# The first head group's inverse roots: eight rows through device memory in place of spreading transposes

## The chip, the cores and the metric

The kernel runs on one core of a Trainium2 chip. A core has a matrix engine (PE in the profile, with PEld for its weight loads), three engines for elementwise work (DVE, ACT and POOL), and an engine that mostly issues transfers (SP). Each engine takes its instructions in order and waits on semaphores for the others. The metric is the device time of one execution in microseconds. Three executions of the kernel before took 1020.29, 1020.35 and 1021.29 us; the median is 1020.35 us.

## The reference

One encoder layer on 1024 tokens of width 1024, all in float32. Two attention groups of eight heads each work on one projection; each group's output is normalised by the root mean square over its 512 columns before the shared output projection. A gated MLP follows. Only the first group's normalisation is touched by the change.

```
hn   = rmsnorm(h, norm_mix)
proj = einsum('bsd,de->bse', hn, w_in)
qa, ka, va, qb, kb, vb = split(proj)
o_a  = window_gqa_sink(rope(qa), rope(ka), va, sink)     # 8 heads of 64, window 128
o_b  = neighbourhood_attention(qb, kb, vb, rpb)          # 8 heads of 64, 16 x 64 grid
mix  = concatenate([rmsnorm(o_a, norm_a), rmsnorm(o_b, norm_b)])
h    = h + einsum('bse,ed->bsd', mix, w_out)
h    = h + conv_gated_mlp(rmsnorm(h, norm_ffn), ...)
out  = rmsnorm(h, norm_final)
```

with `rmsnorm(x, g) = x * rsqrt(mean(x * x) + 1e-6) * g`. For the first group that is, for each token, 1 / sqrt(sum of 512 squares / 512 + 1e-6): 1024 numbers, one for each token.

## The kernel before

Activations are kept transposed: 128 features on the partitions, 1024 tokens along the free axis. `mix[0:4]` are the four tiles of the first group's output, `mix[4:8]` those of the second. Scaling the tiles by a number per token therefore needs that number in all 128 partitions: a tile of 128 x 1024 in which every row is the same. This tile is `norm["a"]` (`rstda` in the profile).

Every float32 product is made of three matmuls with rounded high parts and remainders (`block`, L178 to L180), so PE has much to do. The order of PE's instructions is the order of the program text (`manual_schedule`). On the other engines a planner orders the work: it places each instruction when its inputs are ready by the planner's own reckoning of durations, and among ready ones takes the earlier in the program, with `tc.high_priority(offset=500)` pulling one ahead.

PE's text is an interleaving of two streams. The attention units make scores, transposes and value products. The generator `rest()` yields projection blocks, one k tile for one half of the tokens at a time, and `fill(n)` puts n of these blocks between attention steps. `jobs[i]` are 15 projections (column tiles 3 to 17) followed by eight output projections; a job has 16 blocks, 8 for each half. Small pieces of other work hang on places in this stream: `aux[i, n]` is called after block n of job i, just ahead of the next block. "(12, 5)" below is such a place.

For the first group, these pieces are, in the kernel before:

- (11, 8) `square_a`: `squares` (L193, L195) squares the four `mix` tiles on ACT and adds them on DVE, in halves, into a tile of the pool `t` that has three buffers.
- (12, 2) and (12, 5) `narrow_a`: `add_up` transposes 4 blocks of 128 x 128 of the sum on PE (L204) into a PSUM bank and reduces them on DVE (L205), so that the sums of 512 tokens stand in 4 columns of `norm["v"]`, a tile of 128 x 8. After the second half `inverse_root` (L208) takes the square root on ACT and the reciprocal on DVE.
- (12, 11) and (12, 13) `wide_a`: `widen` makes 4 transposes on PE of a column that is repeated 128 times (L235), which leaves the 512 numbers in every partition of a PSUM bank; ACT copies it to `norm["a"]` (L828).
- (13, 1) to (13, 12) `normed_a`: eight multiplications on DVE, each a half of a `mix` tile (L832).

The PSUM banks of `narrow_a` and `wide_a` carry the tag `pj`, of which there are two. The projection uses the same two: the first half of a job accumulates in one during blocks 0 to 7, the second in the other during blocks 8 to 15, and `evacuate` (L246, DVE) empties each. The scaled tiles are next read in job 14, where `split_part` (L613, L614) makes their high parts and remainders.

Other work of this stretch that is named below: the softmax (L415 on DVE, L419 on ACT, L421, L423 on POOL), the split of the transposed probabilities (`split_pt`, L429 on ACT, L430 on DVE) that the value product reads (L540, L541), the projection weights (loads L163, splits L170 and L171), the bias of the second group (load L485), and the stacking of queries and keys by transfers (L304 to L307). All loads and stackings are issued by SP, in order.

Of the kernel before, what the change touches and what calls it, by code (L numbers as in the profile page):

```python
# [13 lines left out]
F32 = mybir.dt.float32  # L14
F32R = mybir.dt.float32r
AF = mybir.ActivationFunctionType
# [3 lines left out]
D, S, HD = 1024, 1024, 64  # L20
# [37 lines left out]
def hybrid_layer(tc, xT, w_first, w_in, w_out, w_gate, w_up, w_down, small, sink, rpb, consts, rope, out):  # L58
    nc = tc.nc
    with ExitStack() as ctx:  # L60
# [7 lines left out]
        tpool = inner("temps", 3)  # L68
        apool = inner("att", 2)
        spool = inner("stats", 6)  # L70

        slots = {"xg": 16, "op": 14, "mix": 8, "rstd": 1}

        def big(name, tag, dt=F32):
            return lpool.tile([128, S], dt, name=name, tag=tag, bufs=slots[tag])
# [4 lines left out]
        def bank(name, tag):  # L80
            return psum.tile([128, HALF], F32, name=name, tag=tag)

        f32 = lambda ap: ap.bitcast(F32)
        tsl = lambda h: slice(h * HALF, (h + 1) * HALF)
# [48 lines left out]
        ident = cst[:, K_ID:K_ID + 128]  # L133
# [76 lines left out]
        def inverse_narrow(sqs, dim, tag, n=4):  # L210

            ps = bank("ss", tag)
            v = cpool.tile([128, n], F32, name="v4", tag="v4", bufs=4, padded_shape=[128, 4])
            if len(sqs) == 1:
                for c in range(n):
                    nc.tensor.transpose(ps[:, c * 128:(c + 1) * 128], sqs[0][:, c * 128:(c + 1) * 128], ident)
                with tc.high_priority(offset=500):
                    nc.vector.tensor_reduce(v, ps[:, 0:n * 128].rearrange("p (c w) -> p c w", w=128), axis=mybir.AxisListType.X, op=ALU.add)
                    nc.scalar.activation(v, v, AF.Sqrt, bias=eps, scale=1.0 / dim)
            else:  # L220
                for i, sq in enumerate(sqs):
                    for c in range(n):
                        nc.tensor.matmul(ps[:, c:c + 1], sq[:, c * 128:(c + 1) * 128], ones[:, 0:1], start=c == 0 and i == 0,
                                         stop=i == len(sqs) - 1, skip_group_check=True)
                with tc.high_priority(offset=500):
                    nc.scalar.activation(v[:, 0:n], ps[:, 0:n], AF.Sqrt, bias=eps, scale=float(D) / dim)
            with tc.high_priority(offset=500):
                nc.vector.reciprocal(v[:, 0:n], v[:, 0:n])
            return v

        def widen(v, tag, n=4):

            wide = bank("sw", tag)
            for c in range(n):
                nc.tensor.transpose(wide[:, c * 128:(c + 1) * 128], v[:, c:c + 1].to_broadcast([128, 128]), ident)  # L235
            return wide
# [327 lines left out]
        mg, h1, norm = [None] * 8, [None] * KT, {"halves": 0}  # L564
# [187 lines left out]
        live = {"op": 0}  # L752
# [23 lines left out]
        aux = {}  # L776
# [42 lines left out]
                if h == 1:  # L819
                    inverse_root(norm["v"], 512)  # L820

        def wide_a(h):
            def go():
                if h == 0:
                    live["op"] += 1
                    norm["a"] = big("rstda", "op")
                with tc.high_priority(offset=500):
                    nc.scalar.activation(norm["a"][:, tsl(h)], widen(norm["v"][:, 4 * h:4 * h + 4], "pj"), AF.Copy)  # L828
            return go

        def normed_a(i, h):
            return lambda: nc.vector.scalar_tensor_tensor(  # L832
                mix[i][:, tsl(h)], mix[i][:, tsl(h)], col(C_NA + i), norm["a"][:, tsl(h)], op0=ALU.mult, op1=ALU.mult)

        aux[11, 8], aux[12, 2], aux[12, 5], aux[12, 11], aux[12, 13] = square_a, narrow_a, narrow_a, wide_a(0), wide_a(1)
        for i in range(8):
            aux[13, 1 + i + i // 2] = normed_a(*divmod(i, 2))
        filler = rest()
# [242 lines left out]
        for h in range(2):  # L1081
            for d in range(KT):
                if h == 0 and d + 2 < KT:
                    wo.append(load_wo(d + 2, False))
                ps = bank("pj", ("o", "s", "pj")[(h * KT + d) % 3])
# [4 lines left out]
                if h == 1 and d == 1:  # L1090
                    v = inverse_narrow([total[0]], D, "pt")
# [157 lines left out]
        v = inverse_narrow([total[1]], D, "pt")  # L1249
# [196 lines left out]
        sq, todo, vs = {}, [], {}  # L1446
# [59 lines left out]
        for i, (p, j, c) in enumerate(order):  # L1506
# [10 lines left out]
            ps = banks[p, j]  # L1517
# [26 lines left out]
        for k, cols in enumerate(quarters):  # L1544
            for j in (2, 3):
                ps = banks[6, j]
# [111 lines left out]
```

## Time and profile before

| | |
|---|---|
| median of three runs | 1020.35 us |
| profiled execution, whole | 1019.92 us |
| profiled execution, first to last instruction (span) | 1018.1 us |
| granted TensorE clock, mean | 0.997 |
| DVE busy | 834.6 us (82%) |
| ACT busy | 561.4 us (55%) |
| POOL busy | 108.9 us (11%) |
| transfers | 144.94 MB, mean 142 GB/s |

A page of the profile gives for each engine the time in which it was busy; the chain of waits follows the last instruction back through whatever released each step, and so shows the work that set the end. A timeline row has the start in us, the duration in us, the engine, the line of the kernel, the operation and its output and input tiles. A matmul's row lasts longer than the step to the next one, because matmuls overlap; the step is what it costs, and the chain of waits gives the steps.

### The profile page before, as it was taken

What the parts mean: (1) busy time and instruction counts of PE and PEld (TensorE: products, weight loads), DVE (VectorE), ACT (ScalarE), POOL (GpSimd) and SP (SyncE); (2) the same over time, 40 slices, a digit from 0 to 9 for tenths busy, and PEclk for the clock granted to TensorE, in tenths of its full rate; (3) what the DMA queues carried; (4) which work ended last, traced back from release to release, by engine and by line L of the source; (5) the groups of instructions that cost most, each with busy time, mean ns of one, the idle gap of its engine ahead of it and who ended that gap; (6) DMA issues with size and microseconds to landing.
All of it is one profiled execution on the core that took longest, in us unless ns stands there. A gap on an engine that the chain in (4) does not pass through costs nothing.

```text
span 1018.1 us, 14884 instructions
## 1 busy us (share of the span) xinstructions
PE 1008.2 (99%) x5094; PEld 889.8 (87%) x5094; DVE 834.6 (82%) x1570; ACT 561.4 (55%) x1081; POOL 108.9 (11%) x188
## 2 busy tenths in 40 slices
PE   9999999999999999999999999999999999999996
PEld 8898888899988888888888888888888888888886
DVE  7889888768898799999987786786777678986765
ACT  8567776657677554555544443444443645544451
POOL 0233332222252100000000000000000000000002
PEclk9999999999999999999999999999999999999998
DMA  7223022333335356222452333323232699866744
GB/s 294 78 78 96 31 73 63 83 83 83 84 91 158 103 189 226 83 96 70 186 187 93 114 114 114 104 94 122 96 132 87 226 338 326 299 227 232 233 144 166
DMA packets 68221, 144.94 MB, mean 142 GB/s; under 512 B 8241, under 2 KB 18737, under 8 KB 68145
## 3 DMA queue, kind: packets, MB, share of 16 engines
q1 hardware_dynamic: 58064, 118.82, 36.2%
q10 hardware_dynamic: 10080, 25.17, 6.4%
q8 instruction: 40, 0.66, 0.3%
q14 instruction: 37, 0.30, 0.1%
HBM read 103.58 MB, written 28.57 MB: 130 GB/s over the span
## 4 chain that ended last, share of the span: by engine, by line
PE 88%; DVE 5%; ACT 4%; issue 2%; DMA 1%; DVEq 0%; POOL 0%; SPq 0%; ACTq 0%; POOLq 0%
PE x L1017 7%; PE x L1018 7%; PE x L1019 7%; PE dn L1019 7%; PE dn L1017 7%; PE dn L1018 7%; PE pj L178 6%; PE pj L180 6%; PE pj L179 6%; PE y L1017 4%; PE y L1018 4%; PE y L1019 4%; PE s L392 3%; PE z L1017 2%; PE z L1018 2%; PE z L1019 2%
## 5 line engine op out<-in xcount | busy, mean ns | idle before, releaser
L1017 PE MATMUL x<-hg,whi 128*128 128x512 f32 x352 | 133.5, 379 | 0.0
L1018 PE MATMUL x<-hg,whi 128*128 128x512 f32 x352 | 133.4, 379 | 0.0
L1019 PE MATMUL x<-hg,wlo 128*128 128x512 f32 x352 | 133.4, 379 | 0.0
L1017 PE MATMUL dn<-xd,whi 128*128 128x512 f32 (+1 forms) x330 | 120.8, 366 | 0.0
L1018 PE MATMUL dn<-xd,whi 128*128 128x512 f32 (+1 forms) x330 | 120.5, 365 | 0.0
L1019 PE MATMUL dn<-xd,wlo 128*128 128x512 f32 (+1 forms) x330 | 120.5, 365 | 0.0
L419 ACT ACTIVATE p<-p,nm 128x385 f32<-128x385 f32 (+3 forms) x128 | 75.0, 586 | 62.8 <-DVE nm L415 59.9
L991 ACT ACTIVATE whi<-ws 128x512 fp32r<-128x512 f32 (+1 forms) x100 | 60.7, 621 | 73.7 <-DVE ws L1131 14.5
L423 POOL TENSOR_SCALAR p<-p,sm 128x384 f32<-128x384 f32 (+1 forms) x128 | 80.4, 640 | 191.3 <-DVE sm L421 160.4
L178 PE MATMUL pj<-xgh,whi 128*128 128x512 f32 x245 | 99.7, 407 | 0.0
L179 PE MATMUL pj<-xgl,whi 128*128 128x512 f32 x245 | 93.0, 379 | 0.0
L180 PE MATMUL pj<-xgh,wlo 128*128 128x512 f32 x245 | 92.9, 379 | 0.0
L991 ACT ACTIVATE whi<-raw 128x512 fp32r<-128x512 f32 (+1 forms) x102 | 60.9, 610 | 51.4 <-PE x L1018 16.9
L992 DVE TENSOR_TENSOR wlo<-ws,whi 128x512 fp32r<-128x512 f32 (+1 forms) x100 | 66.5, 680 | 19.3 <-ACT whi L991 19.0
L1478 POOL TENSOR_TENSOR h<-h,wide 128x256 f32<-128x256 f32 (+1 forms) x6 | 5.4, 915 | 670.0 <-ACT wide L1474 670.0
L430 DVE TENSOR_TENSOR pl<-pt,ph 128x384 fp32r<-128x384 f32 (+2 forms) x108 | 63.5, 588 | 15.0 <-ACT ph L429 13.3
L1019 PEld LDWEIGHTS x<-hg,wlo 128*128 128x128 f32 x352 | 66.5, 189 | 9.5
L1018 PEld LDWEIGHTS x<-hg,whi 128*128 128x128 f32 x352 | 66.5, 189 | 9.4
L1017 PEld LDWEIGHTS x<-hg,whi 128*128 128x128 f32 x352 | 66.5, 189 | 9.4
L992 DVE TENSOR_TENSOR wlo<-raw,whi 128x512 fp32r<-128x512 f32 (+1 forms) x102 | 66.5, 668 | 7.1 <-ACT whi L991 6.4
L1019 PEld LDWEIGHTS dn<-xd,wlo 128*128 128x128 f32 x330 | 62.5, 189 | 7.7
L1018 PEld LDWEIGHTS dn<-xd,whi 128*128 128x128 f32 x330 | 62.5, 189 | 7.7
(267 smaller groups left out, 2498.7 us busy)
## 6 DMA issues: line engine op xcount, KB each, us to landing
xd<-x SPq DMA_DIRECT2D x77, 256.0 KB, 5.0
raw<-in_w_down_dram SPq DMA_DIRECT2D x72, 256.0 KB, 4.7
raw<-in_w_gate_dram SPq DMA_DIRECT2D x22, 512.0 KB, 3.4
raw<-in_w_up_dram SPq DMA_DIRECT2D x22, 512.0 KB, 3.5
x<-c ACTq DMA_DIRECT2D x22, 512.0 KB, 2.6
raw<-in_w_in_dram SPq DMA_DIRECT2D x30, 256.0 KB, 2.7
raw<-in_w_down_dram SPq DMA_DIRECT2D x36, 192.0 KB, 4.0
x<-t ACTq DMA_DIRECT2D x11, 512.0 KB, 2.6
```

Of the source, the lines that this page charges most:

```text
L178: nc.tensor.matmul(ps, w[0], mv(x[0][:, tsl(h)]), start=first, stop=False)
L179: nc.tensor.matmul(ps, w[0], mv(x[1][:, tsl(h)]), start=False, stop=False)
L180: nc.tensor.matmul(ps, w[1], mv(x[0][:, tsl(h)]), start=False, stop=last)
L392: nc.tensor.matmul(ps[:, 0:n], qs, k[i][:, cs[0] * 128:cs[0] * 128 + n].rearrange("p (s w) -> p w s", s=2), start=i == 0, stop=i == 1)
L419: nc.scalar.activation(p[:, j, 0:e], p[:, j, 0:e], AF.Exp, bias=nm, scale=-1.0, accum_out=sm[:, j:j + 1])
L423: nc.gpsimd.tensor_scalar(p[:, i, 0:m], p[:, i, 0:m], sm[:, i:i + 1], 1.0, op0=ALU.mult, op1=ALU.mult)
L430: mark["rest"] = nc.vector.tensor_tensor(pl[:, 0:n], ps[:, 0:n], f32(ph[:, 0:n]), op=ALU.subtract)
L991: nc.scalar.activation(hi, src, AF.Copy)
L992: nc.vector.tensor_tensor(lo, src, f32(hi[:, :, :]), op=ALU.subtract)
L1017: nc.tensor.matmul(ps, w[0], x[0], start=first and i == 0, stop=False, skip_group_check=True)
L1018: nc.tensor.matmul(ps, w[0], x[1], start=False, stop=False, skip_group_check=True)
L1019: nc.tensor.matmul(ps, w[1], x[0], start=False, stop=last and i == len(ws) - 1, skip_group_check=True)
```

## The change

The sums of squares and their inverse roots are made as before. The four plus four transposes of `widen` and the two ACT copies behind them go. In their place `row_a` makes one transpose of `norm["v"]` (128 x 8 to 8 x 128), ACT copies it to a corner of the tile of the squares, and a transfer on SP's queue writes these 8 rows, 4 KB, to a tile in device memory. `wide_a` then reads the 1024 numbers back, 128 times over, straight into `norm["a"]`, one transfer of 512 KB on SP's queue. The places change: `square_a` from (11, 8) to (11, 4), `narrow_a` from (12, 2) and (12, 5) to (11, 14) and (12, 1), and the new `row_a` and `wide_a` stand at (12, 4) and (12, 7). `normed_a` stays where it was.

```diff
+        spread_pool = ctx.enter_context(tc.tile_pool(name="roots", bufs=1, space=bass.MemoryType.DRAM))
+        roots = spread_pool.tile([8, 128], F32, name="roots")
...
-        def wide_a(h):
-            def go():
-                if h == 0:
-                    live["op"] += 1
-                    norm["a"] = big("rstda", "op")
-                with tc.high_priority(offset=500):
-                    nc.scalar.activation(norm["a"][:, tsl(h)], widen(norm["v"][:, 4 * h:4 * h + 4], "pj"), AF.Copy)
-            return go
+        def row_a():
+            ps, row = bank("row", "pj"), norm["sq"][0:8, 0:128]
+            nc.tensor.transpose(ps[0:8, 0:128], norm["v"], ident)
+            with tc.high_priority(offset=500):
+                nc.scalar.activation(row, ps[0:8, 0:128], AF.Copy)
+                nc.sync.dma_start(roots, row)
+
+        def wide_a():
+            live["op"] += 1
+            norm["a"] = big("rstda", "op")
+            with tc.high_priority(offset=500):
+                nc.sync.dma_start(norm["a"], bass.AP(tensor=roots.tensor, offset=roots.offset, ap=[[0, 128], [1, S]]))
...
-        aux[11, 8], aux[12, 2], aux[12, 5], aux[12, 11], aux[12, 13] = square_a, narrow_a, narrow_a, wide_a(0), wide_a(1)
+        aux[11, 4], aux[11, 14], aux[12, 1], aux[12, 4], aux[12, 7] = square_a, narrow_a, narrow_a, row_a, wide_a
```

## The prediction

> **What bounds the kernel now.** I read the page first, its busy times and the shares of the chain of waits:
>
> ```profile
> span 1018.1 us, 14884 instructions
> PE 1008.2 (99%) x5094; PEld 889.8 (87%) x5094; DVE 834.6 (82%) x1570; ACT 561.4 (55%) x1081; POOL 108.9 (11%) x188
> PE 88%; DVE 5%; ACT 4%; issue 2%; DMA 1%; DVEq 0%; POOL 0%; SPq 0%; ACTq 0%; POOLq 0%
> ```
>
> PE is busy 99% of the span and makes 88% of the chain. An average over stages doesn't say what the changed stretch is worth, so next I cut the neighbourhood of the edit into windows:
>
> ```profile
> core 0: us, PE busy (x) PEld busy (x) DVE busy (x) ACT busy (x) POOL busy (x), PEclk, DMA share, GB/s
> 238.00:250.00 12.00, 12.00 (x70) 10.81 (x69) 9.05 (x23) 9.34 (x22) 2.49 (x4) 1.00 0.46 116
> 250.00:262.00 12.00, 12.00 (x72) 10.81 (x71) 10.33 (x28) 10.02 (x21) 4.55 (x6) 1.00 0.34 100
> 262.00:284.00 22.00, 22.00 (x137) 20.09 (x135) 19.77 (x46) 12.80 (x35) 6.36 (x10) 1.00 0.23 60
> 284.00:312.00 28.00, 27.53 (x159) 24.02 (x158) 25.89 (x62) 21.99 (x54) 11.75 (x14) 1.00 0.44 112
> 312.00:345.00 33.00, 32.91 (x193) 29.37 (x193) 26.91 (x66) 20.72 (x51) 7.97 (x12) 1.00 0.41 125
> ```
>
> From 238 to 284 us PE has no idle time at full clock, while DVE works 86 to 90% from 250 on. So an instruction taken off PE here is worth its step, and DVE and ACT are close enough behind that a wait for them can become PE's. Only behind the edit, from 284 to 345, is PE idle at all: 0.47 + 0.09 = 0.56 us.
>
> Then the PE timeline places the pieces. A transpose group just ahead of a block tells which block it is:
>
> ```profile
> 248.40 0.46 PE L178 MATMUL pj<-xgh,whi 128*128 128x512 f32 x1
> 249.45 0.38 PE L178 MATMUL pj<-xgh,whi 128*128 128x512 f32 x1
> 252.49 0.60 PE L204 MATMUL ss<-cst,sq 128*128 128x128 f32 x4
> 255.64 0.60 PE L204 MATMUL ss<-cst,sq 128*128 128x128 f32 x4
> 258.01 0.48 PE L178 MATMUL pj<-xgh,whi 128*128 128x512 f32 x1
> 259.09 0.38 PE L178 MATMUL pj<-xgh,whi 128*128 128x512 f32 x1
> 262.34 0.60 PE L235 MATMUL sw<-cst,v 128*128 128x128 f32 x4
> 264.79 0.62 PE L235 MATMUL sw<-cst,v 128*128 128x128 f32 x4
> ```
>
> The group at 252.49 is place (12, 2), so block 0 of job 12 starts at 249.45 and block 15 of job 11 at 248.40; 255.64 is (12, 5), 258.01 is block 8 and 259.09 block 9. A block with the attention steps between comes every (259.09 - 249.45) / 9 = 1.07 us here.
>
> What a piece costs PE is its step in the chain of waits:
>
> ```profile
> 258.09 0.41 PE pj L178
> 259.25 0.22 PE pj L178
> 262.51 0.44 PE sw L235 x4
> 264.95 0.46 PE sw L235 x4
> 311.76 0.43 PE o L541
> 316.21 0.11 PE o L541
> ```
>
> **What goes from PE.** The eight spreading transposes: 0.44 + 0.46 = 0.90 us. In their place comes one transpose with 128 moving columns: 0.44 / 4 = 0.11 us. Net 0.79 us less, all of it on the path that sets the end.
>
> A small wait goes too. Block 8 of job 12 took 0.41 us for its first matmul against 0.22 for block 9's: 0.19 us. It opens the second `pj` bank, which `narrow_a`'s second half had held until its reduction ended at 257.29 + 0.67 = 257.96, and PE started at 258.01. Under the change that bank is emptied for the last time by the short copy after (12, 4), four blocks or about 4 us ahead of block 8. Gain 0.19 us; together 0.98 us.
>
> **What ACT, DVE and POOL get.** These rows carry the times:
>
> ```profile
> 243.77 0.69 DVE L195 TENSOR_TENSOR sq<-sq 128x512 f32<-128x512 f32 x1 [1.68 <-ACT sq L193]
> 251.66 0.69 DVE L195 TENSOR_TENSOR sq<-sq 128x512 f32<-128x512 f32 x1
> 253.88 0.68 DVE L205 TENSOR_REDUCE v<-ss 128x4 f32<-128x512 f32 x1
> 257.29 0.67 DVE L205 TENSOR_REDUCE v<-ss 128x4 f32<-128x512 f32 x1
> 259.45 0.20 DVE L208 RECIPROCAL v<-v 128x8 f32<-128x8 f32 x1
> 261.74 0.56 DVE L430 TENSOR_TENSOR pl<-pt,ph 128x384 fp32r<-128x384 f32 x1
> 263.80 1.05 DVE L832 SCALAR_TENSOR_TENSOR mixa<-mixa,par,rstda 128x512 f32<-128x512 f32 x1
> ```
>
> ```profile
> 257.83 1.28 ACT L208 ACT_TABLE_LOAD   x1
> 259.12 0.30 ACT L208 ACTIVATE v<-v,eps 128x8 f32<-128x8 f32 x1
> 263.18 0.58 ACT L828 ACTIVATE rstda<-sw 128x512 f32<-128x512 f32 x1
> ```
>
> ACT loses two copies of 0.58 us and gets one on 8 rows, at most the 0.30 of the small root. That is cost free either way, since ACT is idle for 22.00 - 12.80 = 9.2 us of the window from 262 on; had it no such gap, it would be the 0.30. DVE and POOL keep their instructions.
>
> **The squares, four blocks sooner.** Eight squarings and six additions of 0.69 us move from 242 to 252 us to about 238 to 248, and with them nothing on SP or POOL. The distance to the first `narrow_a` stays ten blocks ((11, 8) to (12, 2) before, (11, 4) to (11, 14) after). It was just enough: the last addition ended at 252.35, the transposes came at 252.49. DVE has gaps at the new place (1.68 us ahead of 243.77), ACT is busy 9.34 of 12 us there. Wait of PE between 0 and 0.8 us (0.8: the addition late by one other instruction of 0.69 and a semaphore); I take 0.1, since the gaps are there.
>
> **The first `narrow_a` one block ahead of a job's start.** This is the new wait that I expect. At (11, 14) the free bank is the one that the first half of job 11 has left; the other still accumulates. Block 15 follows, and block 0 of job 12 then needs a bank: either this one, after its reduction, or the other, after its evacuation. In the kernel before, a `narrow_a` at (12, 2) had six blocks until the next bank was opened. Now: transposes from 248.40 to 248.84; block 15 and a score step lead to block 0 at 249.45 + 0.44 = 249.89. The reduction started 253.88 - 252.49 = 1.39 and 257.29 - 255.64 = 1.65 us after its first transpose and took 0.68, so the bank is free 2.07 to 2.32 us after 248.40, at 250.5 to 250.7. PE would wait 0.6 to 0.8; were DVE free at once, it would be 248.84 + 0.16 + 0.68 = 249.7 and no wait. Range 0 to 0.9; I take 0.5, nearer to the measured delays, because the additions that crowded DVE at 252 are past.
>
> **The row three blocks behind the sums.** Before, `wide_a` came six blocks behind the second `narrow_a` and found its roots ready: the reciprocal ended at 259.65, the group came at 262.34. The chain from first transpose to root is 259.65 - 255.64 = 4.01 us, with a table load of 1.28 in it. The new `row_a` stands three blocks behind: in the trace of before that is from 255.64 to 259.09, or 3.45 us. PE waits 4.01 - 3.45 = 0.56. Bounds: 0, if the reduction starts at once (1.65 - 0.60 = 1.05 us sooner), and 0.56 + 0.58 + 0.69 = 1.8, if ACT and DVE each have one more instruction ahead. I take 0.5. Behind this transpose stands everything on PE, so the wait is paid in full; later in the stretch nothing gives it back.
>
> **The write and the read on SP.** The transfers have no like in this trace, a 4 KB store and a broadcast load. The nearest rows, the last number being the median in us from issue to landing:
>
> ```profile
> x<-c ACTq DMA_DIRECT2D x22, 512.0 KB, 2.6
> xr<-in_xT_dram SPq DMA_DIRECT2D x8, 512.0 KB, 5.6
> h1d<-h ACTq DMA_DIRECT2D x16, 256.0 KB, 3.3
> out_dram<-h SPq DMA_DIRECT2D x13, 128.0 KB, 1.7
> ```
>
> Block 0 of job 12 starts at 249.89 + 0.5 = 250.4, the second `narrow_a` two blocks later at 250.4 + 2 x 1.07 = 252.5, and the root stands at 252.5 + 4.0 = 256.5. Transpose and copy take 0.30 each at most, which makes 257.1; then issue 0.5 (the issues below show 0.52), write 1.7 to 3.3, issue 0.5, read 2.6 to 5.6. The tile lands between 262.4 and 267.0. The write is far smaller than any of these rows and so nearest to the shortest; for the read I take the shorter 512 KB row, since the DMA share is 0.23 in the window where it runs. That is 262.4, where the copies of before allowed the first multiplication at 263.80. Job 14, which reads the result, starts at 284: the cover is 17 us.
>
> The read must wait for the write's landing, and SP's queue stands meanwhile, up to 0.3 + 0.5 + 3.3 = 4.1 us. Queued behind it are the bias load, the stackings and a weight load:
>
> ```profile
> 258.90 0.58 SPq L485 DMA_DIRECT2D rr<-in_rpb_dram  x1
> 264.88 0.52 SPq L163 DMA_DIRECT2D raw<-in_w_in_dram  x1
> ```
>
> The bias is that of the next head, the stackings those of head 5 (whose units begin near 285), the weights those of job 14: each wanted some 20 us later, so I cost this at nothing; without that cover it would be the 4.1 us.
>
> The Trainium skill, "DMA: Bandwidth & Descriptors", in the section "Anatomy of one DMA" (written for the GpSimd path), speaks against such a trip: every transfer has about 2 us that don't depend on its size, because the semaphore fires only after the last byte is confirmed, and this is longest where device memory is the target. By its figures write and read together would take an estimated 2.0 + 2.0 + 1.2 = 5.2 us, where the short rows give 1.7 + 2.6 = 4.3; the landing would be 0.9 us later, and the sum the same.
>
> **Sum.** -0.98 + 0.1 + 0.5 + 0.5 = +0.12 us on the profiled execution's 1019.92 us (its span of 1018.1 and 1.8 around it). That execution is 0.43 us under the median of 1020.35. Forecast: 1020.35 + 0.12 = 1020.5 us, no change. Its own range is that of the three waits, from none, 1019.4, to 0.8 + 0.9 + 1.8 = 3.5 us with all at their upper ends, 1022.9.
>
> **Rivals.**
>
> *All waits hidden.* DVE takes both reductions at once, since the additions are over sooner. Then the whole 0.98 us stays: 1019.4 us. For it speaks the gap of 1.68 us that the squares now fill, against it the 1.05 us that the second reduction waited, behind work that doesn't move.
>
> *The multiplications block DVE (slower).* DVE's order is fixed by a planner that reckons the landing itself. If it puts the first `normed_a` where it believes `norm["a"]` to be ready and the tile is later, DVE stands, with the splits of the probabilities behind. The split at 261.74 ended at 262.30 and its value product came at 264.40:
>
> ```profile
> 264.40 0.27 PE L540 MATMUL o<-ph,v 128*128 128x256 f32 x1
> ```
>
> So PE has 2.1 us of cover, and decides for slower from a stand of 2.1 + 1.8 = 3.9 us on. Were both trips reckoned at nothing, DVE would be sent there at 257.1 and stand until 262.4 to 267.0, 5.3 to 9.9 us. At 5.3 us PE loses 3.2: 1020.5 + 3.2 = 1023.7 us. For it: the first multiplication at 263.80 followed its input's copy (263.18 + 0.58) without a gap, though its place in the text is five blocks on, so the planner does push these forward. Against it: a planner that reckons 1.4 us or more for the two transfers together brings the stand from 5.3 under the deciding 3.9. The rule of the Trainium skill quoted above would make the stand 0.9 us longer.
>
> *A better order behind (faster).* From 284 to 345 PE loses 0.56 us idle, and single value products lose more (0.43 at 311.76 against 0.11 at 316.21: 0.3). With ACT and DVE freer by 1 us and a new order there, three such waits and the idle time could go: -0.98 - 0.56 - 0.9 = -2.4, 1017.9 us. Against it: these waits hang on `split_part` and the softmax, which the change leaves.
>
> *It doesn't do what it says*, if the planner holds the early pieces back; then the waits shift but PE's 0.79 us go all the same. That lies within the forecast's range.
>
> **How the numbers follow.** Forecast 0.36, all hidden 0.16, DVE blocked (or another of the new waits at several times its price) 0.34, better order 0.14. A measurement of this kernel can tell about 0.2%, or 2.0 us, from no change. Then: within 0.52 (the first two), slower 0.34, faster 0.14. The range runs from the better order at 1018.0 to DVE blocked at 1023.8, which leaves out about half of the faster case and a third of the slower one, 0.2 in all.
>
> **What would show it.** Right: seven fewer transposes on PE, none at L235 near 262; a first matmul of job 12's block 0 with a step of 0.5 to 1 us instead of 0.22; a wait of about 0.5 us ahead of the 8-row transpose; `norm["a"]` landing near 262.5 and the multiplications right behind. Wrong: DVE idle for several us with the landing as what ended it; a PE wait over 1 us at any of the three places; or a difference of over 1 us that comes from behind 284, where I expect none.

## The result, and the profile after

| | before | changed |
|---|---|---|
| median of ten runs each | 1020.6 us (1020.12 to 1021.94) | 1023.4 us (1022.78 to 1024.85) |
| ratio | | 1.0027, 95% interval 1.0018 to 1.0035 |
| span of the profiled execution | 1018.1 us | 1021.3 us |

The change costs 2.8 us, 0.27%. The time lies in the predicted range, but the forecast was no change at 1020.5 us, and its own sum allowed at most 1022.9. What came is the slower side, near the 1023.7 us of the rival with the blocked DVE.

The page of the changed kernel shows nothing of it at first sight:

```profile
PE 1008.4 (99%) x5087; PEld 890.0 (87%) x5087; DVE 835.2 (82%) x1570; ACT 560.4 (55%) x1080; POOL 107.6 (11%) x188
```

There are seven matmuls fewer, as the change intends, and yet the busy time of PE is the same to 0.2 us: the total shows neither what was saved nor where PE waits. The windows are clearer, in the same stretches and columns as before:

```profile
238.00:250.00 12.00, 12.00 (x71) 10.90 (x70) 10.59 (x24) 7.28 (x19) 3.08 (x6) 1.00 0.54 133
250.00:262.00 12.00, 9.85 (x57) 8.48 (x56) 8.63 (x21) 9.47 (x20) 3.61 (x6) 1.00 0.47 122
262.00:284.00 22.00, 21.30 (x127) 19.17 (x126) 18.53 (x46) 11.20 (x30) 4.67 (x8) 1.00 0.20 66
284.00:312.00 28.00, 27.74 (x164) 24.68 (x163) 25.58 (x62) 22.05 (x55) 12.66 (x16) 1.00 0.36 91
312.00:345.00 33.00, 32.73 (x190) 28.89 (x189) 27.55 (x67) 21.32 (x55) 9.14 (x14) 1.00 0.46 140
```

PE, which had no idle time from 238 to 284, now has 2.15 us of it in the second window and 0.70 in the third. From 284 to 345 it is idle for 0.26 + 0.27 = 0.53 us, against 0.56 before: the loss is at the edit, not downstream. The view of PE's waits from 240 to 290 names it (line, tile, who released it; us in total, times, longest):

```profile
PE pj L180 <- DVE v L207: 1.2, 1, 1.2
PE row L826 <- DVE v L210: 0.9, 1, 0.9
PE pj L180 <- DVE v L336: 0.7, 1, 0.7
```

In the kernel before this view has no row in these windows. The PE timeline gives the places:

```profile
249.15 0.60 PE L206 MATMUL ss<-cst,sq 128*128 128x128 f32 x4
...
250.40 0.33 PE L394 MATMUL s<-kb,q 128*128 128x384 f32 x1
251.94 0.48 PE L180 MATMUL pj<-xgh,whi 128*128 128x512 f32 x1 [1.22 <-DVE v L207]
...
254.21 0.60 PE L206 MATMUL ss<-cst,sq 128*128 128x128 f32 x4
...
257.25 0.28 PE L394 MATMUL s<-kb,q 128*128 128x256 f32 x1
258.46 0.27 PE L826 MATMUL row<-cst,v 128*8 128x128 f32 x1 [0.94 <-DVE v L210]
258.49 0.46 PE L180 MATMUL pj<-xgh,whi 128*128 128x512 f32 x1
...
277.83 0.33 PE L394 MATMUL s<-kb,q 128*128 128x384 f32 x1
278.87 0.45 PE L180 MATMUL pj<-xgh,whi 128*128 128x512 f32 x1 [0.70 <-DVE v L336]
```

The first is block 0 of job 12, which opens the bank that the first half's sums still hold. A score matmul of 384 columns has a step of 0.16 us where nothing waits (its twin, at 250.24, had it), here 251.94 - 250.40 = 1.54: a loss of 1.38. Its own step is then 0.32 (the next matmul starts at 252.26) where it is 0.22 without a wait (249.45 to 249.67 in the kernel before), another 0.10. The second is the row transpose waiting for its roots: 258.46 - 257.25 = 1.21 against 0.11 for 256 columns, a loss of 1.10. The third is block 8 of job 13, which opens the bank of the value transposes that stand behind block 3 (at 273.55): 278.87 - 277.83 = 1.04 against 0.16, a loss of 0.88. Together 3.36 us, and 3.46 with the longer step.

The DVE timeline says why each bank or root was late:

```profile
250.86 0.42 DVE L432 TENSOR_TENSOR pl<-pt,ph 128x256 fp32r<-128x256 f32 x1 [1.04 <-ACT ph L431]
251.20 0.68 DVE L207 TENSOR_REDUCE v<-ss 128x4 f32<-128x512 f32 x1
...
258.12 0.20 DVE L210 RECIPROCAL v<-v 128x8 f32<-128x8 f32 x1
...
268.44 2.74 DVE L838 SCALAR_TENSOR_TENSOR mixa<-mixa,par,rstda 128x512 f32<-128x512 f32 x4 [0.92 <-DMA rstda<-roots]
...
275.12 1.94 DVE L838 SCALAR_TENSOR_TENSOR mixa<-mixa,par,rstda 128x512 f32<-128x512 f32 x2
276.98 0.41 DVE L336 TENSOR_TENSOR v<-vt,v 128x256 fp32r<-128x256 f32 x1
277.32 0.73 DVE L838 SCALAR_TENSOR_TENSOR mixa<-mixa,par,rstda 128x512 f32<-128x512 f32 x1
277.98 0.41 DVE L432 TENSOR_TENSOR pl<-pt,ph 128x256 fp32r<-128x256 f32 x1
278.31 0.41 DVE L336 TENSOR_TENSOR v<-vt,v 128x256 fp32r<-128x256 f32 x1
```

The first reduction began 2.05 us after the first of its transposes (249.15 to 251.20) although DVE was idle for 1.04 of them: in its order stands a probability split ahead, and that one waited for its high part from ACT. The multiplications began at 268.44, 4.6 us later than before, after DVE had stood 0.92 us for the landing; with them the value splits (L336) of job 13 ended at 278.72, when the bank was wanted at 277.99.

The landing was late because of two more stations. ACT's timeline and SP's issues:

```profile
256.49 1.28 ACT L210 ACT_TABLE_LOAD   x1
...
258.62 1.28 ACT L421 ACT_TABLE_LOAD   x1
259.91 0.51 ACT L421 ACTIVATE p<-p,nm 128x256 f32<-128x256 f32 x1
...
260.42 0.25 ACT L828 ACTIVATE sq<-row 8x128 f32<-8x128 f32 x1
```

```profile
259.76 0.58 SPq L487 DMA_DIRECT2D rr<-in_rpb_dram  x1
260.44 0.55 SPq L308 DMA_DIRECT2D kb<-ka  x1
261.08 0.43 SPq L829 DMA_DIRECT2D roots<-sq  x1
264.93 0.34 SPq L835 DMA_DIRECT2D rstda<-roots  x1
```

The row came from PE at 258.73 and was copied at 260.42, behind the table load for the exponentials and one step of the softmax. The write went out at 261.08, with the bias load of 244.5 KB and a stacking of 256 KB issued just ahead of it. The read could be issued 3.85 us later and took 3.5 us to land, at 268.4.

To see what the stretch costs in all, compare the starts of the same matmul in the two profiled executions. Ahead of the first sums and at the end of the stretch these are, before:

```profile
248.04 0.38 PE L180 MATMUL pj<-xgh,wlo 128*128 128x512 f32 x1
...
279.83 0.33 PE L540 MATMUL o<-ph,v 128*128 128x384 f32 x1
```

and in the changed kernel:

```profile
248.72 0.38 PE L182 MATMUL pj<-xgh,wlo 128*128 128x512 f32 x1
...
283.17 0.33 PE L542 MATMUL o<-ph,v 128*128 128x384 f32 x1
```

The changed kernel enters 0.68 us late and leaves 3.34 us late, so the stretch costs 2.66 us. The 0.68 are older than the change: at 30.39 and 31.04 the first sums of squares (L204 before, L206 changed) already stand 0.65 apart, in code that is the same. The 2.66 us are what the steps give. The spreading transposes are worth 0.85: the lag is 3.18 us ahead of them (261.47 and 264.65) and 2.33 behind them (265.47 and 267.80). So 3.46 of waits less 0.85, less 0.18 for the small wait at block 8 of job 12, plus the row's own 0.11, is 2.54; the last 0.1 are smaller delays near 279 to 281. Behind the stretch the lag falls and rises by up to 0.4 us, and at the end it is 3.3 us.

### The profile page after: what moved, and what is told of

It is laid out like the page before. It is cut to its first block, busy times and chain, and to the rows that moved or that the text cites. A ratio compares the mean times of both kernels' runs of the same rounds, so it can differ in the third digit from the quotient of the medians.

```text
span 1021.3 us, 14875 instructions
## 1 busy us (share of the span) xinstructions
PE 1008.4 (99%) x5087; PEld 890.0 (87%) x5087; DVE 835.2 (82%) x1570; ACT 560.4 (55%) x1080; POOL 107.6 (11%) x188
## 4 chain that ended last, share of the span: by engine, by line
PE 88%; DVE 5%; ACT 3%; issue 2%; DMA 1%; POOL 0%; DVEq 0%; ACTq 0%; POOLq 0%
PE x L1025 7%; PE x L1023 7%; PE x L1024 7%; PE dn L1024 7%; PE dn L1025 7%; PE dn L1023 7%; PE pj L180 6%; PE pj L182 6%; PE pj L181 6%; PE y L1025 4%; PE y L1023 4%; PE y L1024 4%; PE s L394 3%; PE z L1023 2%; PE z L1025 2%
## 5 line engine op out<-in xcount | busy, mean ns | idle before, releaser
L1354 ACT ACTIVATE xd<-xd 128x512 fp32r<-128x512 f32 x77 | 47.2, 626 | 40.2 <-DMA xd<-x 40.1
```

The lines of the kernel that those rows point to most:

```text
L1354: nc.scalar.activation(hi, f32(lo), AF.Copy)
```

## The experiments

Two theories at first. *The waits*: the loss is PE waiting at these three places, each with its own cause. *The trip*: writing and reading back, with SP's queue standing and the landing late, cost it all. The ratios are to the kernel before, run beside each of them; 0.001 is 1 us.

**e1, the places without the trip**, on the kernel before.

```diff
-        aux[11, 8], aux[12, 2], aux[12, 5], aux[12, 11], aux[12, 13] = square_a, narrow_a, narrow_a, wide_a(0), wide_a(1)
+        aux[11, 4], aux[11, 14], aux[12, 1], aux[12, 11], aux[12, 13] = square_a, narrow_a, narrow_a, wide_a(0), wide_a(1)
```

> The kernel before with the squares and sums at the changed places, (11, 4), (11, 14) and (12, 1), and the spreading transposes kept at (12, 11) and (12, 13): no trip through memory. Theory of the waits (the changed kernel's loss is PE waiting at three places: block 0 of job 12 for its bank, the row transpose for its roots, block 8 of job 13 for the bank of the value transposes): the first wait stays, a step of about 1.4 us longer, the 0.19 us at block 8 of job 12 goes, the other two don't arise: 1020.6 + 1.4 - 0.2 = 1021.8 us. Theory of the trip (writing, reading back and the late landing cost it all): no loss, 1020.4 to 1020.6 us.

Measured: 1022.02 us, ratio 1.0014 (1.0005 to 1.0023). Its view of PE's waits from 240 to 290 has one row:

```profile
PE pj L178 <- DVE v L205: 1.2, 1, 1.2
```

The bank wait is there without any transfer, and it alone makes the kernel slower, by 1.2 us or so. The trip does not cost it all.

**e2, the trip without the places**, on the changed kernel.

```diff
-        aux[11, 4], aux[11, 14], aux[12, 1], aux[12, 4], aux[12, 7] = square_a, narrow_a, narrow_a, row_a, wide_a
+        aux[11, 8], aux[12, 2], aux[12, 5], aux[12, 11], aux[12, 13] = square_a, narrow_a, narrow_a, row_a, wide_a
```

> The changed kernel with every piece back at the places of before: squares (11, 8), sums (12, 2) and (12, 5), row (12, 11), read (12, 13). Theory of the waits: neither the bank wait of block 0 nor the row wait arises, PE saves 0.79 us net; the tile lands some 8 us after the row's copy, near 271, and the multiplications may then push the value splits of job 13 (third wait, 0 to 1 us): 1020.6 - 0.8 = 1019.8 us, up to 1020.8. Theory of the trip: as slow as the changed kernel or slower, 1023.4 us and more, since the tile lands later still.

Measured: 1023.71 us, ratio 1.0037 (1.0024 to 1.0049), as the theory of the trip had it. The first two waits are gone, and the third has grown. DVE, then PE:

```profile
273.42 0.75 DVE L838 SCALAR_TENSOR_TENSOR mixa<-mixa,par,rstda 128x512 f32<-128x512 f32 x1 [2.96 <-DMA rstda<-roots]
...
277.47 0.42 DVE L336 TENSOR_TENSOR v<-vt,v 128x256 fp32r<-128x256 f32 x1
```

```profile
278.03 0.45 PE L180 MATMUL pj<-xgh,whi 128*128 128x512 f32 x1 [1.59 <-DVE v L336]
...
281.00 0.38 PE L543 MATMUL o<-pl,v 128*128 128x256 f32 x1 [0.56 <-DVE pl L432]
```

DVE stands 2.96 us for the landing with the probability and value splits queued behind, and PE then waits for both: compared with the same matmuls of before, it falls back by 3.1 us between 265 and 281. So neither theory holds alone: the places make two waits, the trip makes the third.

**e3, everything sooner still**, on the changed kernel, the sums in the bank that stands free in the second half of job 11.

```diff
-        aux[11, 4], aux[11, 14], aux[12, 1], aux[12, 4], aux[12, 7] = square_a, narrow_a, narrow_a, row_a, wide_a
+        aux[10, 14], aux[11, 9], aux[11, 12], aux[12, 2], aux[12, 4] = square_a, narrow_a, narrow_a, row_a, wide_a
```

> The changed kernel with all pieces sooner still, so that both sums use the bank that stands free in the second half of job 11: squares (10, 14), sums (11, 9) and (11, 12), row (12, 2), read (12, 4). Theory of the waits: none of the three, and the tile lands before 263: 1020.6 - 0.98 = 1019.6 us, the best of these. Theory of the trip: SP's queue stands as long as in the changed kernel, 1022 to 1023.4 us.

Measured: 1021.96 us, ratio 1.0014 (1.0005 to 1.0023): not the best, and 2.4 us above what I expected. The first two waits are gone, the third stays, although the tile lands three microseconds sooner. The row of its DVE, of its PE and of its SP:

```profile
265.30 0.75 DVE L838 SCALAR_TENSOR_TENSOR mixa<-mixa,par,rstda 128x512 f32<-128x512 f32 x1 [1.91 <-DMA rstda<-roots]
```

```profile
277.82 0.45 PE L180 MATMUL pj<-xgh,whi 128*128 128x512 f32 x1 [1.48 <-DVE v L336]
```

```profile
256.76 0.31 SPq L829 DMA_DIRECT2D roots<-sq  x1
257.13 0.48 SPq L307 DMA_DIRECT2D q<-kb  x1
257.65 0.59 SPq L309 DMA_DIRECT2D ka<-kb  x1
258.35 0.54 SPq L835 DMA_DIRECT2D rstda<-roots  x1
```

This read took 6.9 us to land, with two stackings of 256 KB issued just ahead of it. The write, with no other transfer issued on its queue in the 1.8 us ahead of it, had landed at the latest when the read was issued, 1.59 us after it. DVE stood 1.91 us, and all eight multiplications still stand ahead of the value splits in its order. An earlier trip was no cure here, since DVE's order counted on a landing earlier yet.

**e4, the value splits first.** On the changed kernel the multiplications are queued on DVE behind the value splits of job 13, and their places in the text go with them, to (13, 4) to (13, 11); nothing else moves.

```diff
-                    nc.vector.tensor_tensor(dst[:, :, 64:128], src, f32(dst[:, :, 0:64]), op=ALU.subtract)
+                    mark["value low"] = nc.vector.tensor_tensor(dst[:, :, 64:128], src, f32(dst[:, :, 0:64]), op=ALU.subtract)
...
-            return lambda: nc.vector.scalar_tensor_tensor(
-                mix[i][:, tsl(h)], mix[i][:, tsl(h)], col(C_NA + i), norm["a"][:, tsl(h)], op0=ALU.mult, op1=ALU.mult)
+            def go():
+                with behind("value low"):
+                    nc.vector.scalar_tensor_tensor(
+                        mix[i][:, tsl(h)], mix[i][:, tsl(h)], col(C_NA + i), norm["a"][:, tsl(h)], op0=ALU.mult, op1=ALU.mult)
+            return go
...
-            aux[13, 1 + i + i // 2] = normed_a(*divmod(i, 2))
+            aux[13, 4 + i] = normed_a(*divmod(i, 2))
```

> The changed kernel with the eight multiplications held on DVE behind the value splits of job 13, nothing else moved. Theory of the waits: block 8 of job 13 finds its bank, 0.84 us come back: 1022.6 us. Against it: the wait only moves to another place, 1023.4 us.

Measured: 1022.04 us, ratio 1.0016 (1.0007 to 1.0024), where the changed kernel had 1.0027. Its waits from 240 to 290:

```profile
PE pj L180 <- DVE v L207: 1.2, 1, 1.2
PE row L826 <- DVE v L210: 0.9, 1, 0.9
PE pj L180 <- DVE t L248: 0.2, 1, 0.2
```

The third wait is gone and has not come back elsewhere, but for 0.2 us. The two intervals overlap; that the 1 us is this wait rests on the trace, and on e5 and e8 below.

**e5, e3 and e4 together.**

> Both former edits in one: all pieces sooner still (squares (10, 14), sums (11, 9) and (11, 12), row (12, 2), read (12, 4)) and the multiplications held behind the value splits of job 13. Theory of the waits: none of the three is left, PE keeps its 0.8 to 1.0 us: about 0.9 us under the kernel before, ratio 0.9991. If the trip costs in another way than through these waits: at or above the kernel before, ratio 1.000 to 1.001.

Measured: 1019.77 us, ratio 0.9993 (0.9984 to 1.0001). PE's waits from 240 to 290 are down to the one of 0.2 us for `t` (L248). From e3's 1.0014 the same hold brought 2 us.

**e6, the hold alone on the kernel before.** The edit of e4 on the kernel before, with its spreading transposes.

> The kernel before, with nothing but the multiplications held behind the value splits of job 13. Theory of the waits: no change, ratio 1.000 (0.9995 to 1.0005), since that bank was free in time there. If holding them helps by itself: ratio 0.9990 or less, and the gain of the other kernels with this edit isn't the removed wait.

Measured: 1020.29 us, ratio 1.0000 (0.9991 to 1.0009). The hold is worth nothing that these runs can tell where nothing is late, so what it brought in e4 and e5 is the removed wait. A small part is not: in e6's trace the same matmuls lag by 0.30 us at 282 (281.89 before, 282.19 here) and by 0.07 at 312 (312.46 and 312.53), so the new order behind the multiplications is worth some 0.2 us by itself.

**e7, the row three blocks later**, on top of e4.

```diff
-        aux[11, 4], aux[11, 14], aux[12, 1], aux[12, 4], aux[12, 7] = square_a, narrow_a, narrow_a, row_a, wide_a
+        aux[11, 4], aux[11, 14], aux[12, 1], aux[12, 7], aux[12, 10] = square_a, narrow_a, narrow_a, row_a, wide_a
```

> The changed kernel with the multiplications held and the row and read three blocks later, at (12, 7) and (12, 10). Theory of the waits: the row finds its roots, a wait of 0.9 to 1.1 us less than in the kernel with the multiplications held alone (1.0016 times the kernel before); the bank wait of 1.4 us stays: ratio 1.0004 to 1.0006. If the row's wait only moves: 1.0016.

Measured: 1022.14 us, ratio 1.0016 (1.0008 to 1.0025), no gain over e4. The row waits no more, but the bank that it lies in is wanted by block 8 of job 12 right behind it, and ACT copies the row out only behind the high parts of a probability split. PE, and ACT:

```profile
260.62 0.48 PE L180 MATMUL pj<-xgh,whi 128*128 128x512 f32 x1 [0.73 <-ACT sq L828]
```

```profile
259.94 0.47 ACT L431 ACTIVATE ph<-pt 128x384 fp32r<-128x384 f32 x1
260.31 0.25 ACT L828 ACTIVATE sq<-row 8x128 f32<-8x128 f32 x1
```

That is 0.73 of the 0.94 us handed on to the next piece. This run also shows a wait of 0.9 us near 357 us, at the second group's spreading transposes, that e4 has not. What released it is the reciprocal of that group's roots (L230); the same wait is 0.2 us in the changed kernel and 0.4 in e10. Why it differs I did not follow.

**e8, e2 and e4 together**: the trip at the places of before, with the value splits first.

> The trip through memory with every piece at the places of before (ratio 1.0037 as it was) and the multiplications held behind the value splits. Theory of the waits: the wait of 1.6 us at block 8 of job 13 and DVE's stand of 3.0 us for the landing go, and with them the further waits for the probability splits: ratio 0.9992 to 0.9998. If the landing still comes too late for DVE: 1.001 or more.

Measured: 1019.75 us, ratio 0.9990 (0.9981 to 0.9998). None of the three waits is left. Against e2 the hold brought 0.0047, nearly 5 us.

**e9, the first sums one block sooner**, on top of e4.

```diff
-        aux[11, 4], aux[11, 14], aux[12, 1], aux[12, 4], aux[12, 7] = square_a, narrow_a, narrow_a, row_a, wide_a
+        aux[11, 4], aux[11, 13], aux[12, 1], aux[12, 4], aux[12, 7] = square_a, narrow_a, narrow_a, row_a, wide_a
```

> The changed kernel with the multiplications held, and the first half's sums at (11, 13) in place of (11, 14). Theory of the waits: block 0 of job 12 waits for a distance, so one block of about 1.05 us more takes the step from 1.38 us too long to 0.3; the row's wait of 1.1 stays: ratio 1.0016 - 0.0010 = 1.0006. If DVE's order, not the distance, sets when the bank comes free (the reduction stays behind the same probability split): wait 1.2 as before, ratio 1.0016.

Measured: 1021.16 us, ratio 1.0005 (0.9995 to 1.0014). Its waits:

```profile
PE row L826 <- DVE v L210: 1.8, 1, 1.8
PE pj L180 <- DVE t L248: 0.2, 1, 0.2
```

One block of distance takes the bank wait away altogether. It does so in two ways at once: the transposes stand a block sooner, and on DVE the reduction (249.40) now goes ahead of the probability split that it stood behind (250.52). This run doesn't tell the two apart. The row's wait grew from 0.9 to 1.8. Its distance from the second transposes is the same 3.15 us, but the chain from them to the roots took 4.95 us (252.42 to 257.37) where it had taken 4.11: DVE came to the second reduction 1.65 us after its transposes and not 0.81. The sum came out as expected, the split between the two waits did not.

**e10, both sums sooner**, on top of e4.

```diff
-        aux[11, 4], aux[11, 14], aux[12, 1], aux[12, 4], aux[12, 7] = square_a, narrow_a, narrow_a, row_a, wide_a
+        aux[11, 4], aux[11, 10], aux[11, 13], aux[12, 4], aux[12, 7] = square_a, narrow_a, narrow_a, row_a, wide_a
```

> The changed kernel with the multiplications held, and the sums at (11, 10) and (11, 13), row and read where the change has them. Theory of the waits: the row stands seven blocks behind the sums and doesn't wait; the second sums' bank is the one block 0 of job 12 needs, a wait of about 0.3 us as in the kernel with the first sums a block sooner; PE keeps 0.7 us: ratio 0.9996. If a row at (12, 4) waits for another thing than its roots (the engines that copy and write it): ratio 1.0006 or more.

Measured: 1019.64 us, ratio 0.9989 (0.9980 to 0.9998). The three waits are gone; the view from 240 to 290 has one row left:

```profile
PE pj L180 <- DVE t L248: 0.2, 1, 0.2
```

The changed kernel with its sums four blocks sooner and the multiplications behind the value splits is faster than both kernels, than the one before by 0.1%, which the interval just leaves clear of no change. e8 reaches the same within the intervals.

## Why the prediction was right and wrong

**What bounds the stretch: right.** PE had no slack from 238 to 284, every wait made there was paid in full, and what was gained and lost behind 284 nearly cancels: the lag is 3.34 us there and 3.3 at the end.

**What goes from PE: right.** The two groups were worth 0.85 us, by the lag ahead of them and behind them, where I had taken 0.90 from the chain of waits. With the row's 0.11 the net is 0.74 us, not 0.79. The 0.19 at block 8 of job 12 came as reckoned (0.18), in e1 too, except where the row's copy is late (e7).

**The squares sooner: right.** No wait ahead of the first sums; the additions were done in time.

**The bank wait at block 0 of job 12: right mechanism, mis-sized.** "Range 0 to 0.9; I take 0.5", measured 1.38, above the range. I took the delays of the kernel before as the worst case and expected less because the additions had left. But DVE's crowding wasn't what decided: it sat idle for 1.04 us with the reduction next in line behind a split that waited for ACT. In a queue with a fixed order a late instruction ahead makes all behind it late.

**The row's wait: right mechanism, mis-sized.** "I take 0.5", measured 1.10. The chain from transposes to roots was 258.32 - 254.21 = 4.11 us, as the 4.01 of before. The distance was smaller: 257.36 - 254.21 = 3.15 us of PE work to the place of the row, not the 3.45 that I had read at another spot of the stream. That spot holds the small wait of 0.19 us at block 8, which I had myself counted as going, and attention steps of 384 columns in place of 256. From the roots' end to the transpose's start there are another 0.14 us.

**The landing: this step failed.** "The tile lands between 262.4 and 267.0 ... I take 262.4"; it landed at 268.4. Of the 6.0 us, 1.8 come from the roots, which stood at 258.3 and not at 256.5. Transpose and copy took 2.35 where I had taken 0.6, since the copy waited 1.7 us behind the table load and a softmax step; 0.4 passed from there to the issue. The write and the read took 3.85 and 3.5 where I had taken 2.2 and 3.1 with their issues. The section "Anatomy of one DMA" of the Trainium skill's page "DMA: Bandwidth & Descriptors" had the right sign: by its figures the two transfers take an estimated 0.9 us more than the 5.3 with issues that I had taken, and they took 7.3. But its reason, a fixed cost of about 2 us that is largest where device memory is written, is not what the runs show: in e3 the write to device memory had landed within 1.59 us. The slow write of the changed kernel stood behind two large transfers of its own queue, and such a wait is in none of my terms.

**The cover of the landing: the error with the largest lesson.** I weighed it against the reader of the result, job 14 with 17 us to spare, and costed the multiplications at nothing there. What is late first is not the reader but DVE's own queue: the multiplications stand ahead of the value splits, whose bank PE wants in block 8 of job 13. The rival of the blocked DVE had this idea, at the wrong victim: I gave it 2.1 us of cover from the probability split, and said that it decides from a stand of 3.9 us. In the changed kernel a stand of only 0.92 us cost PE 0.88, and in e2 one of 2.96 us cost 3.1 in all, since the eight multiplications of 0.74 us move with it.

So the 2.8 us are not the rival's 3.2 at one place, and that the time came out near the rival's 1023.7 is luck. They are three waits, of which I had two in the sum at less than half their size and the third not at all, less 0.74 us of saved PE work and the 0.18 at block 8.

**SP's queue: right.** The read was issued 3.85 us after the write, within the 4.1 that I allowed, and no wait of PE goes back to the transfers behind.

## What to carry to other kernels

When a matrix engine is the bound, count in its own steps how far each producer stands ahead of its consumer, and ask that of every shared resource (here two PSUM banks), not of the data alone. A late input costs first whatever is queued behind its reader on that reader's engine: with the reader moved behind that work, the same slow transfer turned here from 4 us of loss (e2) to 1 us of gain (e8). Only then does the saved work show.

## What the runs showed that I had not expected

- A 512 KB broadcast read of the same 4 KB took 3.5 us to land in the changed kernel and 6.9 us in e3, where two 256 KB stackings had been issued on the same queue up to 1.2 us ahead of it.
- The 4 KB write shows the same. The read behind it was issued 3.1 to 3.9 us after it in the six kernels with two large transfers issued up to 1.4 us ahead of the write (the changed kernel, e2, e4, e7, e8, e9), and 1.6 to 2.2 us after it in the three without (e3, e5, e10). No run changes those transfers alone, so that they are the cause is argued and not shown.
- A copy of 8 rows that takes 0.25 us came 1.7 us after its input, because the return of ACT from the square root to the exponential, with a table load of 1.28 us and one softmax step, stands ahead of it.
- DVE, busy for 72% of the window from 250 to 262 in the changed kernel, began an urgent reduction 2.05 us after the first of its transposes while idle for half of that time.
